# Samples' unit operations on ScalarE and VectorE queued behind the cast and the remainder of the weight granule that precedes them in the program

## The chip, the cores and the metric

One core of one Trainium2 chip runs the whole kernel. The metric is the device time of one execution in microseconds (us); the time of a kernel is the median of several executions. PE is the matrix engine (TensorE), ACT the scalar engine (ScalarE), DVE the vector engine (VectorE), POOL the GpSimd engine, and SP the engine that here only issues DMAs.

## The reference

One inference step of one decoder layer, for a prompt of 256 tokens and for 8 samples of one token each, with the same weights. All data are f32.

```python
def _layer(x, mem_k, mem_v, s_gla, s_conv, s_ffn, lw):
    m, s_gla_new, s_conv_new = _token_mixing(x, mem_k, mem_v, s_gla, s_conv, ...)
    x = _layer_norm(DN_ALPHA * x + m, ln1_g, ln1_b)
    f, s_ffn_new = _conv_ffn(x, s_ffn, w_ffn_gate, w_ffn_up, w_ffn_conv, b_ffn_conv, w_ffn_down)
    x = _layer_norm(DN_ALPHA * x + f, ln2_g, ln2_b)
    return x, s_gla_new, s_conv_new, s_ffn_new

# inside _token_mixing:  x -> one wide projection (w_in) -> q, k, v, g, a_lr, cb, cc, ch, mq, z_a, z_b, z_m
#   (A) gated linear attention, 4 heads, key width 256, value width 512:
S = (jnp.exp(b_last)[..., None] * S + jnp.einsum('bhsk,bhsv->bhkv', kc * jnp.exp(b_last[:, :, None] - bc), vc))
o = (jnp.einsum('bhts,bhsv->bhtv', scores, vc) + jnp.einsum('bhtk,bhkv->bhtv', qc * jnp.exp(bc), S))
#   (B) short gated convolution of 3 taps, then w_conv_out
#   (M) cross-attention, 4 heads, into 256 memory tokens:
logits = jnp.einsum('blhd,bmhd->bhlm', qm, mem_k).astype(f32) * (MEM_HD ** -0.5)
om = jnp.einsum('bhlm,bmhd->blhd', jax.nn.softmax(logits, axis=-1), mem_v)
merged = jax.nn.sigmoid(z_a) * y_a + jax.nn.sigmoid(z_b) * y_b + jax.nn.sigmoid(z_m) * y_m
return merged @ w_o, s_gla_new, s_conv_new
# _conv_ffn:  (silu(dwconv3(x @ w_ffn_gate)) * (x @ w_ffn_up)) @ w_ffn_down
```

For the prompt the memory keys and values are projected in the kernel and the recurrence starts at zero. For each sample they are read: 2 MB of cached memory keys and values, and 2 MB of recurrence state, which is read, multiplied by the query (the sample's output) and written back decayed and updated. Widths: model 2048, memory and convolution 1024, FFN 5504.

## The kernel before, in words

**Weights in granules.** The 256 prompt tokens and the 8 samples form one moving operand of 264 columns. Every weight matrix is streamed once, in granules of 128 x 2 x 512 f32 (512 KB). `granule` (L243) issues the weight DMA on SP into a `ws` tile (L250, four buffers), then the cast `wh` of it to TensorE's format on ACT (L257, three buffers) and the remainder `wl` = `ws` - `wh` on DVE (L258, three buffers). `group` (L261) then runs 24 matmuls per granule: `wh` with the rounded input (L281), `wh` with the input's remainder (L282), `wl` with the rounded input (L283), for four column blocks, which accumulate in four of the five `mm` banks. When a group ends, ACT or DVE reads its four banks out (L846, L929, L933, L1131 and others). A matmul shows two source names, such as `XH,wh` or `T,wh`.

**Ticks, heads and units.** After the matmuls of a granule, `group` calls `tick` (L212). A tick may do three things: run what is due from `later`, advance by one step the generator of a linear-attention head of the prompt (from L588, in the stretch from about 340 to 700 us), and call `pop` (L185), which takes one unit off `queue`. A unit is one piece of the samples' own work:

- key unit (L372, 16 of them): four products of cached keys with the query on DVE (L386); then one softmax unit.
- value unit (L435, 16): two scalings on ACT (L446), two multiply-adds on DVE (L447), and `sum_rows`: a transpose (L412) and a reduction (L414) on DVE.
- sum unit (L727, 32: four heads, eight samples): one scaling on ACT (L736), one multiply-add on DVE (L737), and the same L412 and L414. It reads 512 KB of state into an `S4` tile.
- update unit (L776, 32): it reads the same state again and a broadcast row of values (L780, L782), does two scalings on ACT (L788) and two multiply-adds on DVE (L789) in place, and two ticks later issues the write of the tile (L790).

A unit is popped every 2, 3, 4 or 6 ticks, by stage (`clock[1]`). The loads of a unit are issued by `ahead` (L171), one or two units in advance, each placed on SP behind the DMA of the last granule. `S4` has three buffers, which the units share with a few other tiles.

**What sets the order.** The program text does not fix the order on an engine. A scheduler builds the kernel: it goes through the instructions, and on each engine it takes the next one by priority (weight DMAs, casts and remainders, and some reads of the banks have raised priorities) and by its own estimate of when the operands are there. `tc.issue_after(i)` adds one rule: what is issued inside it stands behind instruction `i` in the order of its engine. Before the change, a unit's operations on ACT and DVE have no such rule; they stand where the scheduler's estimate finds their load landed, which may be many granules ahead of the granule at whose tick the unit is popped. Once built, the order on each engine is fixed: an instruction that waits holds up everything behind it on its engine.

Of the kernel before, what the change touches and what calls it, by code (L numbers as in the profile page):

```python
# [9 lines left out]
F32 = mybir.dt.float32  # L10
# [24 lines left out]
def layer_kernel(ctx, tc, x_prompt, x_sample, mem_prompt, cache_mem_k, cache_mem_v, state_gla, state_conv,  # L35
# [4 lines left out]
    V, S, G, T = nc.vector, nc.scalar, nc.gpsimd, nc.tensor  # L40
# [6 lines left out]
    def nm(base):  # L47
        uid[0] += 1
        return f"{base}_{uid[0]}"
# [110 lines left out]


    queue = []
    staged = []
    clock = [0, 4]
    owed = [0, 0]
# [5 lines left out]
    def ahead(n):  # L171
        k = 0
        for it in queue:
            if it[0] is not None:
                with ExitStack() as behind:
                    if staged:
                        behind.enter_context(tc.issue_after(staged[0]))
                    it[2] = it[0]()
                it[0] = None
            if it[2] is not None:  # L180
                k += 1
            if k >= n:
                break

    def pop():  # L185
        ahead(1)
        it = queue.pop(0)
        it[1](it[2])
        ahead(2)

    gens = []
# [20 lines left out]
    def tick(left):  # L212

        clock[0] += 1
        due()
        step()
        if clock[0] % clock[1] == 0:
            owed[0] = min(owed[0] + 1, CAP)
        if queue and owed[0] and left >= LEFT and clock[0] >= owed[1]:
            owed[0] -= 1  # L220
            owed[1] = clock[0] + min(APART, clock[1])
            pop()

    def flush():
        owed[0] = 0
        while queue:
            pop()
        while waiting:
            due(True)
# [13 lines left out]
    def granule(srcs, n, ncols):  # L243

        lead[0] += 1
        with tc.high_priority(offset=0 if lead[0] <= 8 else 700):
            st = sb.tile([P, n, ncols], F32, tag="ws", bufs=4, name=nm("ws"))
            for a, o in srcs:
                c = a.shape[-1]
                staged[:] = [nc.sync.dma_start(st[:, :, o:o + c], a.rearrange("(k p) c -> p k c", p=P)).ins]  # L250
        with tc.high_priority(offset=0 if lead[0] <= 8 else 450):
            wh = sb.tile([P, n, ncols], F32R, tag="wh", bufs=3, name=nm("wh"))
            wl = sb.tile([P, n, ncols], F32R, tag="wl", bufs=3, name=nm("wl"))
            with ExitStack() as after:
                for i in first.pop(0) if first else []:
                    after.enter_context(tc.issue_after(i))
                S.copy(wh, st)  # L257
                V.tensor_sub(wl, st, wh.bitcast(F32))  # L258
        return wh, wl

    def group(srcs, nk, xh, xl, k0=0, gk=2, before=None, g0=0):  # L261

        ncols = sum(c for _, _, c in srcs)
        nt = (ncols + P - 1) // P
        pts = [ps.tile([P, 512], F32, tag="mm", bufs=5, name=nm("mm")) for _ in range(nt)]
        cuts = ([0] if g0 else []) + list(range(g0, nk, gk))
        for g, e in zip(cuts, cuts[1:] + [nk]):
            n = e - g
            o, lst = 0, []
            for w, c0, c in srcs:  # L270
                lst.append((w[(k0 + g) * P:(k0 + g + n) * P, c0:c0 + c], o))
                o += c
            wh, wl = granule(lst, n, ncols)
            if before is not None:
                before(g, n)
            for j in range(nt):
                cs = slice(j * P, min((j + 1) * P, ncols))
                p = pts[j][0:cs.stop - cs.start, :NT]
                for t in range(n):
                    kt = g + t  # L280
                    T.matmul(p, wh[:, t, cs], xh(kt), start=(kt == 0), stop=False)  # L281
                    T.matmul(p, wh[:, t, cs], xl(kt), start=False, stop=False)  # L282
                    T.matmul(p, wl[:, t, cs], xh(kt), start=False, stop=(kt == nk - 1))  # L283
            tick((nk - g - 1) // gk)
        return [p[:, :NT] for p in pts]
# [171 lines left out]
    for name, w, dst in (("k", w_mem_k[0], o_mk), ("v", w_mem_v[0], o_mv)):  # L457
        mt_ = [big(F32, (P, 1024)) for _ in range(2)]
        for c in range(2):
            pts = [ps.tile([P, 512], F32, tag="mm", bufs=5, name=nm("mm")) for _ in range(2)]  # L460
            for g in range(0, 16, 2):
                wh, wl = granule([(w[g * P:(g + 2) * P, c * 512:(c + 1) * 512], 0)], 2, 512)
                for m in range(2):
                    ms = slice(m * P, (m + 1) * P)
                    for t in range(2):
                        kt = g + t
                        a, b = mh[kt // 4][:, kt % 4, ms], ml[kt // 4][:, kt % 4, ms]
                        T.matmul(pts[m], a, wh[:, t], start=(kt == 0), stop=False)
                        T.matmul(pts[m], a, wl[:, t], start=False, stop=False)
                        T.matmul(pts[m], b, wh[:, t], start=False, stop=(kt == 15))  # L470
                tick(7 - g // 2)
            with soon():
                for m in range(2):
                    (S.copy if m else V.tensor_copy)(mt_[m][:, c * 512:(c + 1) * 512], pts[m])
# [340 lines left out]
    while om_done[0] < 2:  # L815
        if values[0]:
            pop()
        else:
            due(True)
# [74 lines left out]
    for c in range(2):  # L894
# [12 lines left out]
        for j in range(4):  # L907
            i = c * 4 + j
# [180 lines left out]
    for t0, t1 in ((0, 24), (24, 43)):  # L1089
        hh_, hl_ = [], []  # L1090
        for a in range(t0, t1, 4):
# [7 lines left out]
            for j in range(n):  # L1099
                i = a + j  # L1100
# [133 lines left out]
```

## Time and profile before

| what | value |
|---|---|
| time, median of 3 executions | 2032.67 us (2031.08 to 2033.78) |
| the profiled execution's own time | 2035.91 us |
| span of that execution in the profile | 2034.1 us |
| PE busy | 1990.1 us, 98% of the span |
| DVE busy | 1291.0 us, 63% |
| ACT busy | 979.2 us, 48% |
| POOL busy | 171.7 us, 8% |
| granted TensorE clock, mean | 0.991 |
| DMA, mean | 216 GB/s |

The profile is of one execution, and all its numbers are of that one. A line "out<-in" names the tile written and the tiles read. "<-" in brackets names what ended the idle time of the engine before the instruction. In a table by windows, the columns are the window, its length, busy time (and number of instructions) of PE, of PE's weight loads, of DVE, ACT and POOL, then the granted clock, the DMA share and GB/s.

### The profile page before, as it was taken

The page shows a single profiled execution, that of the slowest core. Times are in us where ns is not written, and L with a number is a line of the kernel's source. Part 1 is how long each engine was busy: PE and PEld are TensorE (multiplying, and loading weights), DVE is VectorE, ACT ScalarE, POOL GpSimd, SP SyncE. Part 2 cuts the span into 40 slices and gives each one's busy share as a digit, 9 for nine tenths or more (in the row PEclk, how much of TensorE's full clock was granted, in tenths as well). Part 3 has the DMA queues.
Part 4 walks back from the last instruction along what each step waited for, and adds up shares of the span by engine and source line. Part 5 has one row for each costly group of instructions (what it writes and reads, how often), then busy time and mean ns, then how long its engine had stood idle before and what let it go on. Part 6 is the DMA issues. An engine that isn't in the chain of part 4 may idle for free. (4 is left out here: it accounts for less than half of the span.)

```text
span 2034.1 us, 38169 instructions
## 1 busy us (share of the span) xinstructions
PE 1990.1 (98%) x15696; PEld 1951.3 (96%) x15696; DVE 1291.0 (63%) x1943; ACT 979.2 (48%) x1334; POOL 171.7 (8%) x247
## 2 busy tenths in 40 slices
PE   9999999999999999999999999999999999999996
PEld 8888999999999989999999998999999999999996
DVE  4666686869688665455544777666665546655646
ACT  4433564555564444344444447655554444544432
POOL 5000030303120020100000201000000000000001
PEclk9999999999999999999999999999999999999998
DMA  8796767666667675666666567987886777765752
GB/s 273 254 325 193 245 199 216 199 207 198 204 209 214 218 218 174 179 184 179 182 179 181 175 194 259 302 262 240 258 262 226 254 260 247 229 178 166 232 181 101
DMA packets 234654, 439.95 MB, mean 216 GB/s; under 512 B 22809, under 2 KB 29422, under 8 KB 234216
## 3 DMA queue, kind: packets, MB, share of 16 engines
q1 hardware_dynamic: 228176, 425.48, 66.9%
q0 software_dynamic: 5440, 10.79, 1.7%
q8 instruction: 123, 2.02, 0.4%
q10 hardware_dynamic: 864, 1.25, 0.2%
q14 instruction: 51, 0.42, 0.1%
HBM read 410.76 MB, written 26.85 MB: 215 GB/s over the span
## 5 line engine op out<-in xcount | busy, mean ns | idle before, releaser
L258 DVE TENSOR_TENSOR wl<-ws,wh 128x1024 fp32r<-128x1024 f32 (+2 forms) x651 | 797.1, 1227 | 546.9 <-ACT wh L257 541.9
L257 ACT CAST wh<-ws 128x1024 fp32r<-128x1024 f32 (+2 forms) x651 | 674.0, 1038 | 823.9 <-PE mm L282 721.6
L281 PE MATMUL mm<-XH,wh 128*128 128x264 f32 (+1 forms) x2064 | 595.5, 289 | 5.2 <-ACT wh L257 2.8
L283 PE MATMUL mm<-XH,wl 128*128 128x264 f32 (+1 forms) x2064 | 590.4, 286 | 3.8 <-DVE wl L258 3.8
L282 PE MATMUL mm<-XL,wh 128*128 128x264 f32 (+1 forms) x2064 | 590.4, 286 | 0.0
L281 PE MATMUL mm<-T,wh 128*128 128x264 f32 x1456 | 416.6, 286 | 3.5 <-DVE T L1131 2.2
L283 PE MATMUL mm<-T,wl 128*128 128x264 f32 x1456 | 415.3, 285 | 0.1
L282 PE MATMUL mm<-T,wh 128*128 128x264 f32 x1456 | 414.7, 285 | 0.0
L281 PEld LDWEIGHTS mm<-XH,wh 128*128 128x128 f32 (+1 forms) x2064 | 391.6, 190 | 6.9 <-ACT wh L257 3.0
L283 PEld LDWEIGHTS mm<-XH,wl 128*128 128x128 f32 (+1 forms) x2064 | 389.9, 189 | 4.9 <-DVE wl L258 4.8
L281 PE MATMUL mm<-X1H,wh 128*128 128x264 f32 x1376 | 391.9, 285 | 0.5 <-DVE G L1108 0.2
L282 PEld LDWEIGHTS mm<-XL,wh 128*128 128x128 f32 (+1 forms) x2064 | 391.0, 189 | 0.3
L282 PE MATMUL mm<-X1L,wh 128*128 128x264 f32 x1376 | 391.1, 284 | 0.0
L283 PE MATMUL mm<-X1H,wl 128*128 128x264 f32 x1376 | 390.9, 284 | 0.0
L281 PEld LDWEIGHTS mm<-T,wh 128*128 128x128 f32 x1456 | 275.0, 189 | 5.3 <-DVE T L1131 3.2
L283 PEld LDWEIGHTS mm<-T,wl 128*128 128x128 f32 x1456 | 274.6, 189 | 0.6 <-DVE wl L258 0.6
L282 PEld LDWEIGHTS mm<-T,wh 128*128 128x128 f32 x1456 | 274.8, 189 | 0.0
L281 PEld LDWEIGHTS mm<-X1H,wh 128*128 128x128 f32 x1376 | 259.4, 189 | 1.6 <-DVE G L1108 0.8
L282 PEld LDWEIGHTS mm<-X1L,wh 128*128 128x128 f32 x1376 | 259.0, 188 | 0.2 <-DVE T L1070 0.2
L283 PEld LDWEIGHTS mm<-X1H,wl 128*128 128x128 f32 x1376 | 258.4, 188 | 0.0
L789 DVE SCALAR_TENSOR_TENSOR S<-T,qks,S 128x512 f32<-128x512 f32 x64 | 46.8, 747 | 60.2 <-DMA T<-dv 60.2
L788 ACT ACTIVATE S<-S,eas 128x512 f32<-128x512 f32 x64 | 43.4, 716 | 60.1 <-DMA S<-in_state_gla_dram 60.1
(338 smaller groups left out, 1442.8 us busy)
## 6 DMA issues: line engine op xcount, KB each, us to landing
ws<-in_w_in_dram SPq DMA_DIRECT2D x255, 512.0 KB, 3.9
ws<-in_w_ffn_down_dram SPq DMA_DIRECT2D x84, 512.0 KB, 5.4
ws<-in_w_ffn_gate_dram SPq DMA_DIRECT2D x80, 512.0 KB, 5.1
ws<-in_w_ffn_up_dram SPq DMA_DIRECT2D x80, 512.0 KB, 4.3
S<-in_state_gla_dram SPq DMA_DIRECT2D x64, 512.0 KB, 5.1
ws<-in_w_gla_out_dram SPq DMA_DIRECT2D x32, 512.0 KB, 3.8
ws<-in_w_o_dram SPq DMA_DIRECT2D x32, 512.0 KB, 3.7
out_dram<-S SPq DMA_DIRECT2D x32, 512.0 KB, 4.7
```

The costliest lines, as they stand in the source:

```text
L257: S.copy(wh, st)
L258: V.tensor_sub(wl, st, wh.bitcast(F32))
L281: T.matmul(p, wh[:, t, cs], xh(kt), start=(kt == 0), stop=False)
L282: T.matmul(p, wh[:, t, cs], xl(kt), start=False, stop=False)
L283: T.matmul(p, wl[:, t, cs], xh(kt), start=False, stop=(kt == nk - 1))
L788: S.activation(sg[:, kt], sg[:, kt], AF.Copy, scale=eas[:, h, kt, b:b + 1])
L789: V.scalar_tensor_tensor(sg[:, kt], pb, qks[:, 1, h, kt, b:b + 1], sg[:, kt], ALU.mult, ALU.add)
```

## The change

`granule` keeps the two instructions of its last cast and its last remainder in a list, `split_at`. `pop` runs a unit's work inside `tc.issue_after` for both. So each ACT operation of a unit stands behind the cast, and each DVE operation behind the remainder, of the last granule that precedes the unit in the program. Loads (`ahead`) stay outside of this. No operation of the kernel is added or taken away. The three lines added above move the names: L257 and L258 become L261 (cast and remainder alike), L250 becomes L254, and lines from L261 on are three higher (L736 becomes L739, L789 becomes L792, L1131 becomes L1134). Since ACT's order changes, it loads its function tables 28 times instead of 26 (two more, in the stretch of the heads).

```diff
@@ -160,6 +160,7 @@
     queue = []
+    split_at = []
     staged = []
@@ -185,7 +186,10 @@
     def pop():
         ahead(1)
         it = queue.pop(0)
-        it[1](it[2])
+        with ExitStack() as behind:
+            for i in split_at:
+                behind.enter_context(tc.issue_after(i))
+            it[1](it[2])
         ahead(2)
@@ -254,8 +258,7 @@
             with ExitStack() as after:
                 for i in first.pop(0) if first else []:
                     after.enter_context(tc.issue_after(i))
-                S.copy(wh, st)
-                V.tensor_sub(wl, st, wh.bitcast(F32))
+                split_at[:] = [S.copy(wh, st).ins, V.tensor_sub(wl, st, wh.bitcast(F32)).ins]
         return wh, wl
```

Three places show how the order moves. The first is ACT, near the end of the convolution's input projections (about 740 to 760 us in the profile before). `T_1374_8974` is the product tile of the last of the 32 sum units and `S_1338_8705` its state tile; `T_1356_8836` is the product tile of the unit ahead of it. Before:

```order
L257 CAST wh_8471<-ws_8469 128x1024
L736 ACTIVATE T_1356_8836<-S_1323_8577,qas 128x512
L257 CAST wh_8501<-ws_8499 128x1024
L257 CAST wh_8543<-ws_8541 128x1024
L257 CAST wh_8581<-ws_8579 128x1024
L257 CAST wh_8611<-ws_8609 128x1024
L736 ACTIVATE T_1374_8974<-S_1338_8705,qas 128x512
L257 CAST wh_8641<-ws_8639 128x1024
L257 CAST wh_8671<-ws_8669 128x1024
```

After:

```order
L261 CAST wh_8808<-ws_8806 128x1024
L739 ACTIVATE T_1356_8836<-S_1323_8577,qas 128x512
L261 CAST wh_8844<-ws_8842 128x1024
L932 ACTIVATE G_1348_8797<-mm_8537 128x264
L932 ACTIVATE G_1348_8797<-mm_8538 128x264
L932 ACTIVATE G_1348_8797<-mm_8539 128x264
L261 CAST wh_8874<-ws_8872 128x1024
L932 ACTIVATE G_1348_8797<-mm_8540 128x264
L261 CAST wh_8904<-ws_8902 128x1024
L261 CAST wh_8946<-ws_8944 128x1024
L739 ACTIVATE T_1374_8974<-S_1338_8705,qas 128x512
L261 CAST wh_8982<-ws_8980 128x1024
```

The last sum unit stood behind the cast of `wh_8611`, and stands now behind that of `wh_8946`, ten casts later. On DVE its three operations move likewise, from behind `wl_8612` to behind `wl_8947`. Its load on SP stands where it was.

The second place is DVE at the end of a group of the FFN's down projection (about 1569 us), where the four banks `mm_17416` to `mm_17419` are read out by L1131 and update units stand between. `S_2434_17900` and `S_2390_17514` are state tiles of two update units. Before:

```order
L258 TENSOR_TENSOR wl_17809<-ws_17806,wh_17808 128x1024
L789 SCALAR_TENSOR_TENSOR S_2434_17900<-T_2435_17902,qks,S_2434_17900 128x512
L1131 SCALAR_TENSOR_TENSOR T_1826_12844<-T_1826_12844,mm_17416 128x264
L1131 SCALAR_TENSOR_TENSOR T_1826_12844<-T_1826_12844,mm_17417 128x264
L258 TENSOR_TENSOR wl_17839<-ws_17836,wh_17838 128x1024
L1131 SCALAR_TENSOR_TENSOR T_1826_12844<-T_1826_12844,mm_17418 128x264
L1131 SCALAR_TENSOR_TENSOR T_1826_12844<-T_1826_12844,mm_17419 128x264
L258 TENSOR_TENSOR wl_17869<-ws_17866,wh_17868 128x1024
L789 SCALAR_TENSOR_TENSOR S_2434_17900<-T_2435_17902,qks,S_2434_17900 128x512
```

After:

```order
L261 TENSOR_TENSOR wl_17809<-ws_17806,wh_17808 128x1024
L1134 SCALAR_TENSOR_TENSOR T_1826_12844<-T_1826_12844,mm_17416 128x264
L261 TENSOR_TENSOR wl_17839<-ws_17836,wh_17838 128x1024
L1134 SCALAR_TENSOR_TENSOR T_1826_12844<-T_1826_12844,mm_17417 128x264
L1134 SCALAR_TENSOR_TENSOR T_1826_12844<-T_1826_12844,mm_17418 128x264
L1134 SCALAR_TENSOR_TENSOR T_1826_12844<-T_1826_12844,mm_17419 128x264
L261 TENSOR_TENSOR wl_17869<-ws_17866,wh_17868 128x1024
L792 SCALAR_TENSOR_TENSOR S_2390_17514<-T_2391_17516,qks,S_2390_17514 128x512 x2
```

The unit that stood ahead of the first read of a bank is gone from there; the unit that stands behind `wl_17869` now is one whose tile was loaded two units earlier.

The third place is SP in the same stretch. `S_2454_18089` takes the buffer that `S_2390_17514` had, three tiles earlier. Before:

```order
L250 DMA ws_17995<-in_w_ffn_down_dram 128x2x512
L790 DMA out_dram<-S_2434_17900 128x2x512
L250 DMA ws_18025<-in_w_ffn_down_dram 128x2x512
L250 DMA ws_18055<-in_w_ffn_down_dram 128x2x512
L780 DMA S_2454_18089<-in_state_gla_dram 128x2x512
```

After:

```order
L254 DMA ws_17995<-in_w_ffn_down_dram 128x2x512
L793 DMA out_dram<-S_2390_17514 128x2x512
L254 DMA ws_18025<-in_w_ffn_down_dram 128x2x512
L254 DMA ws_18055<-in_w_ffn_down_dram 128x2x512
L783 DMA S_2454_18089<-in_state_gla_dram 128x2x512
```

The write of `S_2390_17514` stood 21 rows ahead of the load that takes its buffer; now it stands three rows ahead of it. PE's own order is the same but for two small moves of one matmul's distance.

## The prediction

> **What bounds the kernel now.** I read the page's busy times, clock and chain first.
>
> ```profile
> PE 1990.1 (98%) x15696; PEld 1951.3 (96%) x15696; DVE 1291.0 (63%) x1943; ACT 979.2 (48%) x1334; POOL 171.7 (8%) x247
> PEclk9999999999999999999999999999999999999998
> PE 16%; DVE 1%; DVEq 0%; ACT 0%; issue 0%
> L258 DVE TENSOR_TENSOR wl<-ws,wh 128x1024 fp32r<-128x1024 f32 (+2 forms) x651 | 797.1, 1227 | 546.9 <-ACT wh L257 541.9
> L257 ACT CAST wh<-ws 128x1024 fp32r<-128x1024 f32 (+2 forms) x651 | 674.0, 1038 | 823.9 <-PE mm L282 721.6
> ```
>
> PE is busy for 98% of the span, and ACT's casts mostly wait for PE to free a `wh` buffer (721.6 us): PE sets the pace, and only where it stalls is there something to gain. PE's work is the same after the change. So I looked for the 50 us in which PE does less than in a quiet stretch. Columns: window, length, busy time and count of PE, its loads, DVE, ACT, POOL, clock, DMA share, GB/s.
>
> ```profile
> 850.00:900.00 50.00, 50.00 (x414) 50.00 (x413) 25.68 (x30) 21.48 (x26) 4.80 (x4) 1.00 0.64 182
> 750.00:800.00 50.00, 45.51 (x355) 44.98 (x354) 23.80 (x26) 19.62 (x22) 4.80 (x4) 0.93 0.62 184
> 1550.00:1600.00 50.00, 47.77 (x378) 47.34 (x377) 25.80 (x27) 19.49 (x22) 0.00 (x0) 0.97 0.69 232
> 1350.00:1400.00 50.00, 49.65 (x406) 49.23 (x405) 31.56 (x48) 26.90 (x40) 0.00 (x0) 1.00 0.78 248
> 1500.00:1550.00 50.00, 49.95 (x411) 49.73 (x410) 30.15 (x47) 26.23 (x39) 0.00 (x0) 1.00 0.79 257
> 1600.00:1650.00 50.00, 49.83 (x404) 49.18 (x403) 27.01 (x31) 21.41 (x23) 0.00 (x0) 1.00 0.73 244
> 1650.00:1700.00 50.00, 49.71 (x405) 49.08 (x404) 25.01 (x28) 21.86 (x25) 0.00 (x0) 1.00 0.74 248
> ```
>
> A quiet window has 414 matmuls, 50 / 414 = 0.1208 us each; a granule of 24 takes 2.9 us. The next two windows miss 59 and 36 matmuls (7.1 and 4.35 us), the last four 8, 3, 10 and 9, together 30 (3.6 us). The timeline shows why; first around 755 us:
>
> ```profile
> 740.15 0.46 SPq L731 DMA_DIRECT2D S<-in_state_gla_dram  x1
> 746.17 1.05 ACT L257 CAST wh<-ws 128x1024 fp32r<-128x1024 f32 x1 [4.80 <-PE mm L282]
> 753.13 0.72 ACT L736 ACTIVATE T<-S,qas 128x512 f32<-128x512 f32 x1 [5.91 <-DMA S<-in_state_gla_dram]
> 753.75 2.92 ACT L257 CAST wh<-ws 128x1024 fp32r<-128x1024 f32 x3
> 753.88 0.75 DVE L737 SCALAR_TENSOR_TENSOR T<-S,qas,T 128x512 f32<-128x512 f32 x1 [5.37 <-ACT T L736]
> 754.84 0.50 PE L281 MATMUL mm<-XH,wh 128*128 128x264 f32 x1 [2.76 <-ACT wh L257]
> 757.29 0.59 PE L283 MATMUL mm<-XH,wl 128*128 128x264 f32 x1 [1.74 <-DVE wl L258]
> DMA to landing us min/median/max: 3.8/4.7/13.0
> ```
>
> The last sum unit's load is issued at 740.15 and lands 13.0 us later. Its L736 is already at the head of ACT and waits 5.91 us; three casts are queued behind it and run in one burst afterwards. On DVE three remainders queue behind L737, L412 and L414. PE waits 2.76 us for a cast and 1.74 us for a remainder, and the clock falls (0.93 over the window). The second place, at 1569 us:
>
> ```profile
> 1566.53 1.34 ACT L788 ACTIVATE S<-S,eas 128x512 f32<-128x512 f32 x2 [2.81 <-DMA S<-in_state_gla_dram]
> 1568.55 0.75 DVE L789 SCALAR_TENSOR_TENSOR S<-T,qks,S 128x512 f32<-128x512 f32 x1 [3.57 <-DMA T<-dv]
> 1569.22 0.76 DVE L1131 SCALAR_TENSOR_TENSOR T<-T,mm 128x264 f32<-128x264 f32 x2
> 1569.69 0.39 PE L281 MATMUL mm<-T,wh 128*128 128x264 f32 x1 [2.20 <-DVE T L1131]
> ```
>
> Here an update unit, queued ahead of the reads of the banks, waits for its load; PE needs a bank, and waits 2.20 us. Units that are at the head of their engines before their data are there are common:
>
> ```profile
> ACT S L788 <- DMA S<-in_state_gla_dram: 60.1, 27, 4.1
> ACT T L736 <- DMA S<-in_state_gla_dram: 15.6, 5, 5.9
> DVE S L789 <- DMA T<-dv: 60.2, 20, 4.9
> ```
>
> Most cost PE nothing: casts run up to three granules ahead, and a wait of up to about 4 us (the 4.1 of L788) passes unseen where no read of a bank or second lateness comes on top.
>
> **The change part by part.** *Waits for loads.* Behind their own granule, the units start later than now: the last sum unit ten casts later, 10 x 2.9 = 29 us. L736 came to the head of ACT at 753.13 - 5.91 = 747.2 us; it will come there at about 776, and its load, at the same place on SP, has landed by 753.1 even at 13.0 us. Update units move later too (at 1569 us the one behind `wl_17869` is now that of a tile loaded two units earlier), so I take the three rows of waits to go to nearly nothing.
>
> *755 us:* all 7.1 us were behind that one load; I take 7.1. *1569 us:* no unit stands ahead of the first read of a bank any more, and the reads follow one, then a remainder, then three. The two reads that used to come first took 0.76 us together, so one more of them behind the remainder is late by its 1.22 us at most, against the 2.9 us granule during which PE works through its other banks: nothing. I take 4.35 us. *The 3.6 us of the four other windows* lie around the same kind of waits, but no PE wait there is long enough to be named and some records may be missing; between 0 and 3.6 I take half, 1.8 us.
>
> *What the moves cost.* The same operations run, only elsewhere:
>
> ```profile
> L736 ACT ACTIVATE T<-S,qas 128x512 f32<-128x512 f32 x32 | 22.8, 718 | 15.6 <-DMA S<-in_state_gla_dram 15.6
> L737 DVE SCALAR_TENSOR_TENSOR T<-S,qas,T 128x512 f32<-128x512 f32 x32 | 26.9, 841 | 12.5 <-ACT T L736 12.5
> L412 DVE STREAM_TRANSPOSE T<-T 128x512 f32<-128x512 f32 x48 | 33.9, 707 | 0.8
> L414 DVE TENSOR_REDUCE T<-T 128x16 f32<-128x512 f32 x48 | 32.7, 681 | 1.0
> L789 DVE SCALAR_TENSOR_TENSOR S<-T,qks,S 128x512 f32<-128x512 f32 x64 | 46.8, 747 | 60.2 <-DMA T<-dv 60.2
> ```
>
> A sum unit is 0.72 us on ACT and 0.84 + 0.71 + 0.68 = 2.2 us on DVE, an update unit 2 x 0.75 = 1.5 us on DVE. A granule's cast and remainder take 1.04 and 1.23 us of 2.9, so in a quiet stretch 1.9 us of ACT and 1.7 us of DVE are free per granule, and the lead of three granules hides the 0.5 us by which a sum unit exceeds this: nothing, unless other work is queued with it. That is so in the heads' stretch, 340 to 700 us, where DVE is nearly full:
>
> ```profile
> 550.00:600.00 50.00, 47.57 (x385) 46.63 (x384) 46.14 (x80) 29.91 (x41) 15.68 (x28) 1.00 0.69 204
> 450.00:500.00 50.00, 47.35 (x370) 46.28 (x370) 45.23 (x76) 33.90 (x48) 17.69 (x27) 0.97 0.62 192
> 469.00 0.39 PE L283 MATMUL mm<-XH,wl 128*128 128x264 f32 x1 [0.52 <-DVE wl L258]
> 471.05 0.39 PE L281 MATMUL mm<-XH,wh 128*128 128x264 f32 x1 [1.30 <-DVE T L846]
> 472.53 0.59 PE L281 MATMUL mm<-XH,wh 128*128 128x264 f32 x1 [0.27 <-DVE T L846]
> ```
>
> DVE's order around these three waits is not changed, so they stay: 0.52 + 1.30 + 0.27 = 2.1 us, and (1 - 0.97) x 50 = 1.5 us of clock, 3.6 us in all. One new crowded place costs between 0 and such 3.6 us; I take 0.5, the row of the shortest single DVE lateness (0.52), since the rate of units is the same and most places are no fuller. The two added table loads on ACT fall in the same stretch, where ACT is busy for 30 to 34 us of 50; bounded above by the same 0.52, taken as nothing.
>
> *SP.* The state tiles are held longer, and the write of an update tile now stands just ahead of the load that reuses its buffer.
>
> ```profile
> out_dram<-S SPq DMA_DIRECT2D x32, 512.0 KB, 4.7
> ws<-in_w_ffn_down_dram SPq DMA_DIRECT2D x84, 512.0 KB, 5.4
> SPq L250 <- DVE wl L258: 1123.1, 489, 6.4
> ```
>
> A weight load waits for the remainder four granules back, so SP moves one load per granule. The write goes out 1.5 us behind its remainder (two L789), two weight loads follow, and the tile load stands 2 x 2.9 - 1.5 = 4.3 us behind the write, which lands in 4.7: SP is held 0.4 us, inside the 2.9 us until it may issue the next weights. Nothing. Were this cover gone, weights issued four granules ahead (11.6 us) that land in 5.4 us and need 1.04 + 1.23 us on ACT and DVE still have 3.9 us to spare.
>
> **Sum:** 7.1 + 4.35 + 1.8 - 0.5 = 12.75 us. The profiled execution took 2035.91 us (span 2034.1), so after the change such a one would take about 2023.2. It lies 3.24 us above the median of 2032.67; from the median the same step gives **2019.9 us**.
>
> *The clock* is part of these sums: with gaps of 2.76 and 2.20 us the granted clock was 0.93 and 0.97 over the two windows, (0.07 + 0.03) x 50 = 5 us of PE time at the lower clock.
>
> **Rivals.** *(a) Only a part of it comes.* For: the 13.0 us landing is one of 32 (median 4.7), and the profiled execution is 3.24 us above the median, so the stall at 755 may not be in every timed execution; or new small waits at the reads of the banks eat the small gains. Then 4.35 + 1.8 and some of 7.1, say a third (2.4), less 0.5: 8.0 us, 2024.6 us. Against: the order on each engine is fixed, and a load of even 9 us would hold the casts.
>
> *(b) Nothing happens.* The lateness is not in the order but in the stretch: the casts that PE missed would be late through their own weights, or a bank's read takes the place of the unit at 1569 us (4.35 us back) and 755 us is an accident of the profiled execution (7.1 back). Then 1.8 - 0.5 is left: about 2031.4 us. For: weights and tiles share the queues, so what delayed a tile by 8 us may delay them. Against: ACT's row at 753.13 names the tile, and behind it three casts run without a gap, so their weights were there.
>
> *(c) Slower: the heads' stretch chokes.* Units that used to slip into a free place on DVE are now tied to a remainder, where a head's own operations are queued too. Each place where DVE gets more than about 4 us behind costs 3.6 us by the rows of 469 to 472. With most of the 32 sum units in that stretch, six of them (6 x 3.6 = 21.6 us) would turn the gain into 12.75 + 0.5 - 21.6 = 8.4 us lost, 2041.0 us; it decides from four such places on. For: DVE is 92% busy there. Against: the units' number per window is the same, and a unit adds 2.2 us at once, less than 4.
>
> *(d) Slower: SP is held by the tile buffers.* If the writes of update tiles land as late as the 13.0 us of that one load, SP is held 13.0 - 4.3 = 8.7 us, 5.8 beyond the free 2.9, and the weights come 1.9 us later than their 3.9 to spare. With 1.5 us of clock that is 3.4 us each; from four of 32 on the gain is gone, and with eight it is 27 us, 2047 us. The median of 4.7 speaks against it.
>
> *(e) The clock's dips stay.* If those dips had another cause than the gaps, these 5 us would not come back: 2024.9 us. For: the gap of 1.30 us at 471 also stands in a window of 0.97, so length alone does not set the dip. Against: the quiet windows have 1.00, and the two places with the long gaps have the dips. [...]
>
> **Chances.** Forecast 0.60, (a) 0.16, (e) 0.03, (b) 0.12, (c) 0.06, (d) 0.03. A measurement of this kernel can tell some 0.2%, 4 us, from no change. Forecast, (a) and (e) are faster by more than that: 0.79. (b) is within it: 0.12. (c) and (d) are slower: 0.09. The time of the likeliest is 2019.9 us. The range reaches down by the small stalls' other half (1.8), no new cost (0.5) and the spread of the runs (1.6), to 2016, and up past (a) with one crowded place (3.6) and half of (b)'s case: 2016 to 2030.
>
> **What would show it.** In the profile after: no L736 or L788 (now L739, L791) waiting for its DMA, at most a few us where 75.7 stood, and L792 not for the row of values; the window 750 to 800 us with 410 or more matmuls and clock 1.00; 1550 to 1600 likewise; the waits of 469 to 472 still there. Wrong would be: PE waits for a remainder or a bank with unit operations just ahead of them on DVE (c); SP waiting long for the writes of update tiles and casts waiting for `ws` (d); a PE stall at 755 or 1569 with the units' loads long landed (b).

## The result, and the profile after

The changed kernel takes 2023.17 us (median of 6 executions, 2021.31 to 2026.64). The kernel before, run beside it and with its earlier runs, takes 2033.72 us (6 executions, 2031.08 to 2039.15). The ratio is 0.9949, with a 95% interval of 0.9939 to 0.9959: faster by about 0.5%, 10.5 us between the medians. The profiled execution took 2023.61 us (span 2021.8) against 2035.91 (2034.1), 12.3 us less.

The page of the changed kernel: busy times, clock, and the chain that ended last.

```profile
PE 1985.2 (98%) x15696; PEld 1949.2 (96%) x15696; DVE 1296.9 (64%) x1943; ACT 982.5 (49%) x1336; POOL 173.8 (9%) x247
PEclk9999999999999999999999999999999999999998
PE 60%; DVE 1%; ACT 0%; issue 0%; DVEq 0%
```

The work is the same; PE is again what bounds the kernel, and the chain now runs back through PE alone for 60% of the span. The windows of the changed kernel that answer to those shown of before, and two more (columns as there: window, length, busy time and count of PE, its loads, DVE, ACT, POOL, clock, DMA share, GB/s):

```profile
150.00:200.00 50.00, 47.95 (x309) 43.64 (x308) 32.35 (x77) 19.73 (x40) 3.50 (x6) 1.00 0.68 213
250.00:300.00 50.00, 47.60 (x367) 47.34 (x366) 38.89 (x70) 28.90 (x45) 13.20 (x21) 0.93 0.65 190
750.00:800.00 50.00, 47.48 (x385) 46.63 (x384) 28.51 (x33) 20.47 (x23) 10.11 (x6) 1.00 0.70 193
1350.00:1400.00 50.00, 50.00 (x413) 50.00 (x413) 31.59 (x48) 27.42 (x40) 0.00 (x0) 1.00 0.85 271
1500.00:1550.00 50.00, 50.00 (x413) 50.00 (x413) 31.83 (x49) 27.31 (x40) 0.00 (x0) 1.00 0.81 269
1550.00:1600.00 50.00, 50.00 (x412) 50.00 (x412) 27.85 (x32) 21.56 (x23) 0.00 (x0) 1.00 0.78 252
1600.00:1650.00 50.00, 50.00 (x412) 50.00 (x412) 25.18 (x26) 21.09 (x23) 0.00 (x0) 1.00 0.81 259
1650.00:1700.00 50.00, 50.00 (x413) 50.00 (x412) 30.78 (x45) 25.18 (x34) 0.00 (x0) 1.00 0.80 241
```

The five windows from 1350 us on now hold 412 or 413 matmuls. They held 406, 411, 378, 404 and 405, so 59 more, 59 x 0.1208 = 7.1 us. The window at 750 us holds 385 instead of 355, 3.6 us, and is still 29 short of the quiet 414. The window at 250 us holds fewer, 367 instead of 379 at a lower clock; a second profile of the same kernel holds 392 there (last section), so this is not the change's work.

What is left at 775 us is a new stall. The changed kernel's timeline there, of ACT, DVE, PE and POOL:

```profile
767.77 1.05 ACT L261 CAST wh<-ws 128x1024 fp32r<-128x1024 f32 x1 [2.82 <-DMA ws<-in_w_conv_out_dram]
772.93 1.05 ACT L261 CAST wh<-ws 128x1024 fp32r<-128x1024 f32 x1 [3.82 <-DMA ws<-in_w_conv_out_dram]
776.28 0.72 ACT L739 ACTIVATE T<-S,qas 128x512 f32<-128x512 f32 x1
...
777.55 0.74 DVE L740 SCALAR_TENSOR_TENSOR T<-S,qas,T 128x512 f32<-128x512 f32 x1
779.68 0.76 DVE L936 TENSOR_TENSOR G<-G,mm 128x264 f32<-128x264 f32 x2
...
775.29 0.39 PE L286 MATMUL mm<-T,wl 128*128 128x264 f32 x1 [0.75 <-DVE wl L261]
780.16 0.39 PE L284 MATMUL mm<-XH,wh 128*128 128x264 f32 x1 [1.20 <-DVE G L936]
782.41 0.39 PE L284 MATMUL mm<-XH,wh 128*128 128x264 f32 x1 [0.54 <-DVE G L936]
...
750.92 5.27 POOL L983 DMA_DIRECT2D S<-in_state_ffn_conv_dram  x2 [5.23 <-DVE T L740]
```

The last sum unit (L739 at 776.28, where the working put it, "at about 776") waits for nothing any more. Nor does any other sum or update unit: in this profile no L739, L791 or L792 waits for a load, where L736 and L788 waited 75.7 us and L789 60.2 us before. But now the casts ahead of it wait for their weights, and the unit then stands between a late cast and the reads of the banks (L936). The last row names another piece of work: POOL's load of the FFN's convolution state, 344 KB in rows of 512 bytes. The transfers issued around it, before (725 to 760 us):

```profile
S<-in_state_gla_dram SPq DMA_DIRECT2D x2, 512.0 KB, 13.0
S<-in_state_ffn_conv_dram POOLq DMA_DIRECT2D x2, 172.0 KB, 17.2
```

and after (750 to 790 us):

```profile
ws<-in_w_conv_out_dram SPq DMA_DIRECT2D x5, 512.0 KB, 8.7
S<-in_state_ffn_conv_dram POOLq DMA_DIRECT2D x2, 172.0 KB, 20.1
```

Before, this load was issued at 730 and 743 us and fell together with the last sum unit's tile, which took 13.0 us. After, it waits for a tile that a sum unit frees (DVE T L740), so it starts at 751 us, and what it meets is weights. (The last number of a row is the median of the landings on record in that window: for the tile it is one of two, for these weights one of five.) The one landing of these weights on record took 8.7 us, and the two casts above wait 2.82 and 3.82 us for them. This suggested that the stall at 755 us had a cause that the prediction had not named, and the experiments begin there.

### The profile page after: what moved, and what is told of

Read it like the earlier page. It is cut to its first block, busy times and chain, and to the rows that moved or that the text cites. A ratio compares the mean times of both kernels' runs of the same rounds, so it can differ in the third digit from the quotient of the medians.

```text
span 2021.8 us, 38114 instructions
## 1 busy us (share of the span) xinstructions
PE 1985.2 (98%) x15696; PEld 1949.2 (96%) x15696; DVE 1296.9 (64%) x1943; ACT 982.5 (49%) x1336; POOL 173.8 (9%) x247
## 4 chain that ended last, share of the span: by engine, by line
PE 60%; DVE 1%; ACT 0%; issue 0%; DVEq 0%
PE mm L285 20%; PE mm L284 20%; PE mm L286 19%; PE sm L726 1%; DVE YT L1196 0%; DVE YT L1202 0%; PE sm L1146 0%; DVE T L1047 0%; DVE yst L1149 0%; ACT L932 0%; ACT L773 0%; DVE T L1171 0%; DVE T L1170 0%; DVE wl L261 0%; PE mm L1044 0%; DVE T L1034 0%
## 5 line engine op out<-in xcount | busy, mean ns | idle before, releaser
L261 DVE TENSOR_TENSOR wl<-ws,wh 128x1024 fp32r<-128x1024 f32 (+2 forms) x651 | 800.0, 1230 | 609.3 <-ACT wh L261 608.5
L261 ACT CAST wh<-ws 128x1024 fp32r<-128x1024 f32 (+2 forms) x651 | 676.1, 1039 | 896.6 <-PE mm L285 784.1
L473 PE MATMUL mm<-wh,T 128*128 128x512 f32 x128 | 51.1, 399 | 0.0
```

The source lines that it names most:

```text
L261: split_at[:] = [S.copy(wh, st).ins, V.tensor_sub(wl, st, wh.bitcast(F32)).ins]
```

## The experiments

Each was timed beside the kernel before on the same chip. Ratios are to the kernel before, with their 95% intervals.

**Which units matter.** A unit gets a kind, and only the units of one kind are issued behind the split:

```diff
-            for i in split_at:
+            for i in split_at if it[3] in BEHIND else []:
```

with BEHIND holding sum units, update units, or key, softmax and value units.

> Only the 32 sum units stand behind the cast and remainder of their granule; key, softmax, value and update units as before the change. Theory: the gain has two separate sources, the last sum unit at 755 us and the update units between 1350 and 1700 us. Then the window 750 to 800 us has about 385 matmuls as in the profile after (355 before), the windows 1350 to 1700 us are as before (378 in 1550 to 1600), and the time is about 3.6 us under the kernel before. Rival: the late weights in 758 to 773 us (row load on POOL) cost what the unit's order gains, so nothing is gained: within 1 us.

> Only the 32 update units stand behind their granule's cast and remainder. Theory: the windows 1350 to 1700 us are as in the profile after (412 or 413 each, 60 matmuls more than before, 7.2 us), 750 to 800 us stays at about 355, and the time is about 7 us under the kernel before; with sum_only it adds up to the whole change (about 10.5 us). Rival: the stretch gains less than its windows show, because what PE saves there it waits for later (writes of the tiles hold SP): under 4 us.

> Only key, softmax and value units (100 to 330 us) stand behind their granule's cast and remainder. Theory: nothing beyond 2 us either way: the wait for L386 at 195 us falls from 2.5 to about 1.3 us, the wait for L414 at 275 us stays at 2.4. Rival: the second half window of lower clock behind 275 us that the profile after shows (6.8 us at half instead of 3.4) belongs to this change: 1.7 us slower there, so no gain or a small loss in all.

| kernel | ratio | interval | 750 to 800 us | 1550 to 1600 us |
|---|---|---|---|---|
| sum units only | 0.9976 | 0.9966 to 0.9987 | 382 | 403 |
| update units only | 0.9976 | 0.9966 to 0.9987 | 360 | 413 |
| key, softmax, value units only | 0.9999 | 0.9989 to 1.0009 | 349 | 407 |
| the whole change | 0.9949 | 0.9939 to 0.9959 | 385 | 412 |

(The last two columns are matmuls in a window of the profile.) The theory of two separate sources holds: each gives 0.24%, about 4.9 us, and together 0.48%, within the noise the 0.51% of the whole change. The update units gave 4.9 us and not 7; their windows were fully repaired, so it is the loss in a typical execution that is smaller than in the profiled one. In the four other profiles in which these units were not moved, 1350 to 1700 us holds 2855 to 2871 matmuls, where the profile of before has 2830 and the changed kernel 2890: 2.3 to 4.2 us lost instead of 7.2. The early units are worth nothing either way. PE's idle time from 150 to 200 us, 50 less its busy time, is 2.98 us with their rule alone and 3.17 before (the wait of 2.51 us at 195 us is part of that), and 250 to 300 us holds 379 matmuls as before. Both places differ between executions: the changed kernel itself has 2.05 us and 367 matmuls in one profile, 2.88 us and 392 in the other.

**What made the stall at 755 us.** In the kernel before, without any unit moved, the two bursts of rows are placed about 100 us later:

```diff
-            G.tensor_tensor(merged[c][:, j], merged[c][:, j], sg[:, j], ALU.add)
+            merge_add = G.tensor_tensor(merged[c][:, j], merged[c][:, j], sg[:, j], ALU.add).ins
     for u in range(2):
-        G.dma_start(fr[u * NF:(u + 1) * NF], state_ffn_conv[0, :, u].rearrange("b (k f) -> k b f", f=P))
+        with tc.issue_after(merge_add):
+            G.dma_start(fr[u * NF:(u + 1) * NF], state_ffn_conv[0, :, u].rearrange("b (k f) -> k b f", f=P))
```

> The kernel before, with one other edit: the two POOL loads of the FFN's convolution state (rows of 512 bytes) stand behind the last merge addition on POOL, about 100 us later; no unit is moved. Theory: these loads slow the DMA queues, and by that the last sum unit's load (13.0 us) in the kernel before; without them it lands in about 5 us, L736 waits under 1 us, PE's waits at 755 us (2.76 and 1.74 us) are gone: about 7 us under the kernel before, with no unit's order changed. Rival: the unit stands too far ahead in ACT's order anyway, and waits 3 us or more: no more than 3 us gained. Second rival: the landing of 13.0 us has another cause and stays: no change.

The time is 0.9995 (0.9985 to 1.0005): no change. Taken alone that would fit the second rival; the profile says otherwise. The windows of this kernel, one wait of ACT, and the timeline where the rows now are:

```profile
750.00:800.00 50.00, 50.00 (x414) 50.00 (x413) 24.74 (x27) 20.27 (x22) 4.79 (x4) 1.00 0.58 178
850.00:900.00 50.00, 45.73 (x350) 45.21 (x350) 22.70 (x27) 18.32 (x23) 10.01 (x6) 0.93 0.69 185
...
747.42 0.73 ACT L736 ACTIVATE T<-S,qas 128x512 f32<-128x512 f32 x1 [1.41 <-DMA S<-in_state_gla_dram]
...
873.98 1.05 ACT L257 CAST wh<-ws 128x1024 fp32r<-128x1024 f32 x1 [6.60 <-DMA ws<-in_w_in_dram]
...
880.60 0.59 PE L281 MATMUL mm<-XH,wh 128*128 128x264 f32 x1 [3.52 <-ACT G L950]
```

The stall has left 755 us entirely (414 matmuls; the last sum unit, still at its early place in ACT's order, waits 1.41 us and costs PE nothing) and stands whole at 870 to 880 us (350), where no unit is, and where a cast waits 6.60 us for its weights. The sum units' loads now land within 5.5 us, where the slowest took 13.0. So the theory that the rows delay the tile was right, and the expected gain failed for a reason that it had missed: in its new place the burst delays the weights that are loaded beside it.

**Spreading the rows.** In the kernel before, and in the changed kernel, 16 small loads on SP take the place of the two bursts:

```diff
-    for u in range(2):
-        G.dma_start(fr[u * NF:(u + 1) * NF], state_ffn_conv[0, :, u].rearrange("b (k f) -> k b f", f=P))
+    def load_rows(b, u):
+        with tc.issue_after(staged[0]):
+            nc.sync.dma_start(fr[u * NF:(u + 1) * NF, b], state_ffn_conv[0, b, u].rearrange("(k f) -> k f", f=P))
+
+    for i in range(2 * NS):
+        later(1 + i, lambda i=i: load_rows(i // 2, i % 2))
```

> The kernel before, with one other edit: the two POOL loads of the FFN's convolution state (1376 rows of 512 bytes in two bursts) become 16 loads of 43 rows on SP, one behind each of 16 weight loads of w_o (about 1110 to 1160 us). No unit is moved. Theory (a): the burst of small rows is what makes PE stall for about 7 us, wherever it stands; spread out it fits into what weights have to spare. Then 750 to 800 us has 410 or more matmuls, 850 to 900 us too, no new stall stands between 1100 and 1200 us, and the time is about 7 us under the kernel before. Rival (b): the small rows cost the same in small pieces, the stall is only cut up and moves to 1110 to 1160 us: within 2 us of the kernel before.

> The changed kernel with the same spreading of the FFN's convolution state rows. By (a) the waits at 775 to 782 us (0.75, 1.20, 0.54 us; about 29 matmuls missing, 3.5 us) go: about 3.5 us under the changed kernel, 14 us under the kernel before; and the change itself is then worth only what the update units give, about 5 to 7 us over before_rows_spread. By (b): no better than the changed kernel.

> The changed kernel with the two bursts of rows in one piece behind the last merge addition on POOL (about 850 us), where no unit stands. By (a) PE stalls there by about 7 us as it did with the kernel before and the same edit (350 matmuls in 850 to 900 us), and no longer at 775 to 782 us: about 3.5 us over the changed kernel, 7 us under the kernel before. If the sum unit in its new place had made the stall at 775 us, it would stay, and the time would be 7 us over the changed kernel.

(The rows are 688, two for each of 8 samples in 43 pieces; the 1376 in that text is a slip.)

| kernel | ratio | interval | 750 to 800 us | 850 to 900 us |
|---|---|---|---|---|
| before, rows spread | 0.9968 | 0.9958 to 0.9977 | 412 | 413 |
| changed, rows spread | 0.9940 | 0.9924 to 0.9956 | 412 | 413 |
| changed, rows later in one piece | 0.9972 | 0.9960 to 0.9983 | 412 | 361 |

Theory (a) holds in all three. Spread out, the rows cost nothing that shows: 1100 to 1150 us, where they stand, has 412 matmuls before and 413 after. That alone takes 0.32%, 6.5 us, off the kernel before, without moving a unit. With the rows out of the way the change is worth 0.9968 to 0.9940, some 0.28%, about what the update units gave alone. And put back in one piece at 850 us they take from the changed kernel what it had gained at 755: the sum units' gain in the change is a gain of place. Against the changed kernel the spread version is lower by its median (2020.94 against 2023.17 us), but the intervals overlap.

Pieces and queue had changed together, so the bursts were also put on SP unspread, right behind the first weight loads of w_o, and the changed kernel was run again beside it:

```diff
+    def load_rows():
+        with tc.issue_after(staged[0]):
+            for u in range(2):
+                nc.sync.dma_start(fr[u * NF:(u + 1) * NF], state_ffn_conv[0, :, u].rearrange("b (k f) -> k b f", f=P))
+
+    later(1, load_rows)
```

> The changed kernel with the rows of the FFN's convolution state in two bursts as before, but on SP, right behind the first two weight loads of w_o (about 1115 us). The spread version had changed two things at once, the pieces and the queue. If the burst of small rows is the cause, PE stalls by 3 to 7 us behind 1115 us, casts there wait for their weights, and the time is that of the changed kernel or 3 us over it. If POOL's queue is the cause, no stall stands there, and the time is that of the spread version, about 3 us under the changed kernel.

> The changed kernel itself, beside the run above on the same chip: about 0.995 of the kernel before, with the stall of about 3.5 us at 775 to 782 us again, since it follows from the order and the burst and not from one execution.

The bursts on SP give 0.9981 (0.9972 to 0.9989), the changed kernel again 0.9957 (0.9944 to 0.9971). The window and the casts of the kernel with the bursts on SP:

```profile
1100.00:1150.00 50.00, 44.45 (x349) 43.81 (x349) 28.88 (x27) 17.32 (x22) 11.74 (x4) 0.97 0.51 174
...
1131.48 1.05 ACT L261 CAST wh<-ws 128x1024 fp32r<-128x1024 f32 x1 [5.11 <-DMA ws<-in_w_o_dram]
1141.07 1.04 ACT L261 CAST wh<-ws 128x1024 fp32r<-128x1024 f32 x1 [8.54 <-DMA ws<-in_w_o_dram]
```

And what the DMA engines did from 1110 to 1150 us, in 40 slices of 1 us (busy tenths and GB/s), with the two weight loads that SP issues behind the bursts:

```profile
DMA  1870771049200000049300000006999999999993
GB/s 37 242 272 16 256 240 33 6 145 285 94 13 22 22 22 22 22 134 319 121 23 22 22 22 22 22 22 217 244 310 358 346 383 371 401 412 395 369 328 117
...
1118.84 7.82 SPq L254 DMA_DIRECT2D ws<-in_w_o_dram  x1
1127.40 8.94 SPq L254 DMA_DIRECT2D ws<-in_w_o_dram  x1
```

64 matmuls are missing (7.7 us) and a cast waits 8.54 us. It is the burst and not POOL's queue. Nor is it the number of bytes: twice, for 6 and 7 us, the core moves only 22 GB/s (412 at most in the same row), and the busy share of its 16 DMA engines stands at 0 tenths, under 0.1 (one busy engine of 16 would give 1/16 = 0.06). By that rate one burst of 172 KB takes about 8 us (an estimate), and a piece of 21.5 KB about 1 us. Meanwhile SP takes 7.82 and 8.94 us to issue the next weights, where the median of a weight load is 0.37 us (L254 in the changed kernel). With the bursts on POOL's queue SP's issues stay short (0.37 us each, from 750 to 790 us in the changed kernel) and the transfers land late (8.7 us for the one weight load on record there), so the harm does not come about in the same way. Whether the short rows are dear, or the 43 partitions of the tile that each load writes, was not tried.

The changed kernel's second profile holds 384 matmuls from 750 to 800 us, where the first holds 385: the stall belongs to the order and the burst, not to one execution. The loss with the bursts on SP is larger than the 3 us expected at most, 5.5 us between the medians: PE misses 64 matmuls there, against 29 at 775 us.

**Which engine's rule.** The changed kernel with the rule for one engine alone:

```diff
-                split_at[:] = [S.copy(wh, st).ins, V.tensor_sub(wl, st, wh.bitcast(F32)).ins]
+                split_at[:] = [S.copy(wh, st).ins, V.tensor_sub(wl, st, wh.bitcast(F32)).ins][1:]
```

(and [:1] for the other).

> The changed kernel, with the rule for VectorE alone: a unit's DVE operations stand behind the remainder, its ACT operations where the scheduler puts them (L788 mostly ahead, as before the change). Theory: between 1350 and 1700 us PE was stopped through DVE, where an update unit stood ahead of the reads of the banks; ACT's waits of up to 4 us for the tile cost nothing. Then L788 (here L791) still waits some 60 us in all for its loads, the windows 1350 to 1700 us have 412 or 413 matmuls each, and the time is that of the changed kernel within 2 us. Rival: it is the casts held on ACT behind L788 that cost PE; then these windows fall back to 400 to 408 and the time is 4 us or more over the changed kernel.

> The changed kernel, with the rule for ScalarE alone: a unit's ACT operations stand behind the cast, its DVE operations where the scheduler puts them (almost everywhere the same place, since they need ACT's result). From dve_only, which was slower than before, the theory is now that the casts held on ACT behind a waiting L788 are what costs PE. Then ACT waits for no state tile, the windows 1350 to 1700 us have 412 or 413 matmuls, and the time is that of the changed kernel within 2 us. Rival: both rules are needed, and the time is 3 us or more over the changed kernel.

With DVE's rule alone the kernel is slower than before: 1.0026 (1.0014 to 1.0038). With ACT's rule alone it is the changed kernel: 0.9951 (0.9939 to 0.9963), with no wait of a unit's scaling for its tile and 412 to 414 matmuls in each window from 1350 to 1700 us. The kernel with DVE's rule alone, at its worst place (waits of ACT, the landing of the tiles that L783 loads, the timelines of ACT and PE, SP's wait):

```profile
ACT S L791 <- DMA S<-in_state_gla_dram: 75.0, 27, 6.1
DMA to landing us min/median/max: 5.9/7.3/9.5
...
1480.65 1.34 ACT L791 ACTIVATE S<-S,eas 128x512 f32<-128x512 f32 x2 [6.14 <-DMA S<-in_state_gla_dram]
1481.89 1.98 ACT L261 CAST wh<-ws 128x1024 fp32r<-128x1024 f32 x2
...
1482.97 0.39 PE L284 MATMUL mm<-X1H,wh 128*128 128x264 f32 x1 [0.65 <-ACT wh L261]
1485.90 0.39 PE L284 MATMUL mm<-X1H,wh 128*128 128x264 f32 x1 [0.91 <-DVE G L1111]
...
SPq L783 <- DMA out_dram<-S: 23.6, 23, 2.1
```

The rival was right, and more strongly than it had said: ACT waits 75.0 us for tiles (60.1 before), up to 6.1 at once instead of 4.1, and that passes what the casts' lead covers (PE then waits 0.65 us for a cast); then remainders and reads of banks are late in their turn (windows 1450 to 1550 us fall to 369 and 383 matmuls). A likely reason is that DVE's half of a unit was moved back, so that a tile's buffer comes free later: SP waits in 23 cases for the write of a tile before it may load the next (23.6 us; 1.7 us in 3 cases before), while ACT's half still stands early. The changed kernel has 18.0 us of such waits without loss, since its ACT operations stand later. This is argued from the rows; these tiles also take longer to land (median 7.3 us; 5.6 for the same load before, 6.3 in the changed kernel), and why was not tried. The rule on ACT moves DVE's half along by itself, since it needs ACT's result.

**A version that adds to it.** The spread version, with the small matmuls that add up a set of units (L423, on which PE waits 2.40 us at 275 us) due later:

```diff
-            later(3, product)
+            later(5, product)
```

> The changed kernel with the rows of the FFN's convolution state in 16 loads on SP (as after_rows_spread), and the small matmuls that sum a set of units (L420 before, L423 now) due five ticks instead of three after the last unit of the set. PE waits there 2.40 us at 275 us for L417, and the clock is at half for 3.4 to 6.8 us behind it. Expected: this wait goes, and with it the lower clock at 275 us (366 or 379 matmuls in 250 to 300 us become about 392), 3.5 to 5 us under after_rows_spread, 16 us under the kernel before. Rival: what needs the sums (the memory branch's output, the heads' norm) then waits in its turn, and nothing is gained.

The time is 0.9927 (0.9915 to 0.9939), 2019.88 us by its median, under both kernels: its interval lies below the changed kernel's second (0.9944 to 0.9971) and meets the first at 0.9939. From the spread version without the later sums (0.9940, 0.9924 to 0.9956) it cannot be told apart, so that the later sums add anything is not shown. From 250 to 300 us PE is idle for 2.30 us (50 less its busy time of 47.70; 2.40 us before), with 378 matmuls and a clock of 0.97 (379 and 0.97 before). The rival was right there that nothing is gained; what PE waits for was not shown.

## Why the prediction was right, and where it was not

The forecast was 2019.9 us, 12.75 us less; measured were 2023.17 us and 10.5 us less. In the profiled executions, on which the sum was made, about 2023.2 us was worked out and 2023.61 measured. That these lie so close is luck in part: the places that the sum names gave 7.1 + 3.6 = 10.7 us, where it had 13.25, and the rest of the 12.3 us came from windows that it does not name. There 150 to 200 us gained 11 matmuls, 700 to 750 gained 5 and 250 to 300 lost 12, and the first and the last of these differ between executions of one kernel. Step by step:

- **1569 us (4.35 us) and the four windows around it (1.8 of 3.6):** the mechanism was right. Together they came to 7.1 us in the profile, since the windows taken at half came in full. In timed executions they are smaller, about 4.9 us by the kernel with the update units alone: the profiled execution had lost more in this stretch than the four other profiles with these units in their old places.
- **755 us (7.1 us):** mis-sized, 3.6 us came in the profile (in timed executions the sum units alone gave 4.9 us, 2.6 to 6.9 by the interval). The step that failed is "The last sum unit's load is issued at 740.15 and lands 13.0 us later", taken as a property of that load, to be outwaited by a unit that comes 29 us later. The unit did outwait it. But the 13.0 us were the work of the burst of rows beside it, and this burst came later too, as it needs a tile that the sum units free, and met weights instead. Rival (b) had the mechanism ("what delayed a tile by 8 us may delay them") and was put aside with a row that shows only that the weights of that moment were there.
- **The cost of the moves (0.5 us):** too small to be seen, and rival (c) did not come. The waits of 469 to 472 us are still there, and the five windows from 400 to 650 us hold 1986 matmuls before and 1987 after.
- **SP:** the load does stand behind the write, at 18.0 us in 15 cases, up to 3.3 each; up from 1.7 us in 3 cases; the 0.4 us of the working was too small, and the cover that it named was enough. Rival (d) did not come:

```profile
SPq L783 <- DMA out_dram<-S: 18.0, 15, 3.3
```

- **The clock:** the dips at 755 and 1569 us went with the gaps, as counted, against rival (e): 0.93 and 0.97 over the two windows before, 1.00 in both after. The longer dip at 275 us is one of that execution (below).
- **"It lies 3.24 us above the median":** an offset of one execution, carried over to the changed kernel. With more runs the median of before is 2033.72, and the changed kernel's profiled execution lies only 0.44 us above its own. The 2.8 us between the two offsets are most of the 3.3 us between the forecast and the median.

## What to carry to other kernels

A work item that an engine reached before its data held what stood behind it there: before, L736 waited 5.91 us for its tile, and three casts ran behind it in one burst. Tie such an item to a later step, on the engine that does its first operation. Here the rest followed (0.9951 with ACT's rule alone), and tying only the later half was worse than nothing (1.0026), probably because it holds the buffers (SP waited 23.6 us for them) while the first half still waits (75.0 us). And where a single transfer lands late, ask what else was being moved beside it before ordering the work around it: here two loads of 344 rows cost PE 3.5 to 7.7 us at each of the places where they were put, and in 16 pieces of 43 rows beside the weights they cost nothing that shows.

## What the runs showed of the hardware that was not expected

Two loads of 344 rows of 512 bytes, 344 KB in all, cost PE 3.5 to 7.7 us on POOL's queue and 7.7 us on SP's (29 to 64 matmuls missing in a window of 50 us). On POOL's queue one tile of 512 KB beside them landed after 13.0 us and one weight load after 8.7 (medians 4.7 for those tiles and 4.2 for weights). On SP's queue the core moved 22 GB/s for 6 to 7 us at a time, with a busy share of its DMA engines under 0.1, and two weight loads behind took SP 7.82 and 8.94 us to issue.

The same wait of PE cost different amounts of clock. From 250 to 300 us PE is idle for 2.39 or 2.40 us, 50 less its busy time, in every profile but that of the last version (in the profiles of before and after in one wait of 2.40 us at about 275 us). The changed kernel had there 0.93 in one profile (the row of 250 to 300 us above) and 1.00 in the other:

```profile
250.00:300.00 50.00, 47.61 (x392) 47.34 (x391) 40.70 (x71) 29.49 (x46) 16.12 (x24) 1.00 0.64 201
```

25 matmuls, 3 us, lie between two executions of one kernel. In slices of 0.5 us, the granted clock in the profiles of before and after falls between 50 and 2000 us at these places alone, and stands there at 0.50 for 3.4 or 6.8 us:

| place | PE's waits, us | at 0.50, us: before | after |
|---|---|---|---|
| 275 us | 2.40 in both | 3.4 | 6.8 |
| 469 to 472 us | 0.52, 1.30, 0.27 before; 0.52, 1.31, 0.49 after | 3.4 | 3.4 |
| 755 us | 2.76, 1.74 before; none after | 6.8 | none |
| 1569 us | 2.20 before; none after | 3.4 | none |

A stretch of 3.4 us at half clock loses 1.7 us, 0.03 of a window of 50 us (an estimate from these numbers), so clocks of 1.00, 0.97 and 0.93 fit none, one and two such stretches. The length of one wait does not set the number: behind the 2.51 us at 195 us before, longer than that at 275 us, the clock stays at 1.00. What sets it was not tried.
